# The end of a decoder layer on one core: read-back of routed rows ahead of the last pair's weights, its down weights by halves, three token tiles summed in PSUM, the last norm by halves on VectorE

## The chip, the cores and the metric

The kernel runs on one core of one Trainium2 chip. The metric is the time of one execution in device microseconds (us); the time of a kernel is the median of its runs.

## The reference

One decoder layer for 512 tokens of width 1024 in float32: a mixer (attention heads beside a short convolution), then a mixture of experts. The change touches only the end of the second part. Each token takes two of 32 experts (width 256), besides a shared expert that all tokens take; the sum is normed and added to the residual stream.

```python
a = jnp.einsum('nd,edf->nef', t, w_gate)
b = jnp.einsum('nd,edf->nef', t, w_up)
hid = jax.nn.silu(a) * b * combine[:, :, None]
routed = jnp.einsum('nef,efd->nd', hid, w_down)
shared = (jax.nn.silu(t @ w_sh_gate) * (t @ w_sh_up)) @ w_sh_down
ffn = routed + shared
h = h + rms_norm(ffn, post_ffn_norm)      # mean square over the 1024 columns, eps, gain
```

## The kernel before

The routed experts are worked off in 16 pairs (j, j+16), the loop of `pairs_gen` (L1445). A pair takes up to 64 tokens of each of its experts; the tokens' rows are gathered from HBM, transposed, and held as one 128-row tile. The weights of an expert are three loads of 1 MB: (e, 0) and (e, 1) hold the two halves of the depth of gate and up together, (e, 2) the down weights. `col2` (L1308) multiplies the two experts side by side, each in 64 of TensorE's columns. For one pair:

- gate and up: 16 float32 matmuls into the bank `pgu`, 8 for the loads (e, 0) and 8 for (e, 1);
- `hidden` (L1281): silu on ScalarE, then the product with the routing weight on VectorE; `hidden_t` (L1285): two transposes on TensorE (`pht`) and a copy on ScalarE; `xpose` (L1274): the next pair's rows transposed;
- `down` (L1515): 4 matmuls for each half of 512 columns, into `pdn`.

What follows differs. For the pairs ahead of `first = NP - PE_PAIRS` (L1444) the result is copied to `yb` and scattered by token to a DRAM buffer `y_d` (`send`, L1510, on POOL). `y_d` has two rows for each token and is read back at the end in four loads `kk0` to `kk3` of 1 MB, one for each tile c of 128 tokens. For the last `PE_PAIRS` pairs, 2 here, `y_out` (L1293) splits the result into a high and a low float32r part (`ys`: a copy on ScalarE, a subtraction on VectorE), and `combine` (L1297) multiplies both by a one-hot matrix `sel` into a bank `pcb`, which VectorE adds to the token's sum `acc(c)` (the tiles `sho`). So a pair's combination is 16 matmuls and 8 additions: 2 halves of the columns by 4 tiles.

`last_gen` (L1521) ends the kernel: it adds the read-back to `acc`, multiplies the last pair's down weights, and combines tile by tile. For the tiles in `INJ` (L47; only tile 3) the sum is not added by VectorE: `acc(c)` is put into a bank `pca` by a float32 matmul with the identity `ident`, and the two products with `sel` accumulate onto it. `post` (L1548) then takes, for each tile and half, the sum of squares on ScalarE and the product with the gain `gp` (into `tm`), which goes to VectorE or to GpSimd (G) by an estimate of the two engines' progress (`M_BIAS`, L1555). The power -0.5 runs on POOL, VectorE multiplies and adds the residual `hb`, and SP stores each half.

All weights pass through one ring of slots, and all their loads are issued by SP in the order of one list, written at L391 to L411:

```python
if j == NP - 1 and i == 2:
    queue_load("gp", g_post[None, :].to_broadcast([P, D]), D)
    for c in range(NT):
        queue_load(f"kk{c}", y_d[:, :].rearrange("(k c p) d -> c p k d", k=2, c=NT)[c],
                   ok=lambda: "sent" in cv)
for e in g:
    queue_load((e, i), we[e, i])
```

A load waits for the slot's last reader and for the landing of the load eight before it. On the other engines the order of the work is fixed when the program is built: generators yield until the builder's own clock (`Progress`) says that their inputs are there, and the one that can go on is taken, by priority. Each engine then runs its list in that order.

Of the kernel before, what the change touches and what calls it, by code (L numbers as in the profile page):

```python
# [46 lines left out]
INJ = (3,)  # L47
M_BIAS = 5.0
F_ALT = ()
# [9 lines left out]
PE_PAIRS = 2  # L59
# [109 lines left out]
def hymba_kernel(ctx: ExitStack, tc: tile.TileContext, xT, xmT, x, meta, cpk, pos, wqkv, wconv, wuq, wukv,  # L169
# [229 lines left out]
    for j, g in enumerate(pairs):  # L399
        for i in range(3):  # L400
            if j == NP - 1 and i == 2:
                queue_load("gp", g_post[None, :].to_broadcast([P, D]), D)
                for c in range(NT):
                    queue_load(f"kk{c}", y_d[:, :].rearrange("(k c p) d -> c p k d", k=2, c=NT)[c],
                               ok=lambda: "sent" in cv)
            for e in g:
                queue_load((e, i), we[e, i])
# [1025 lines left out]
    def pairs_gen():  # L1433
# [11 lines left out]
        for j, es in enumerate(pairs):  # L1445
            ps = None
            for i in range(2):
# [8 lines left out]
                rel(*w)  # L1456
            hidden(ps, wgt[:, j:j + 1], sg, hd)
# [11 lines left out]
            if j > first:  # L1469
                yield flag(sh, "done")  # L1470
                for c in range(NT):
                    yield every(at(ys), free_bank())
                    combine(ys, sel, HALF[0], c)
            yield every(at(hd), free_bank())
            hidden_t(hd, ht)
            if j > first:
                for c in range(NT):
                    yield free_bank()
                    combine(ys, sel, HALF[1], c)
# [8 lines left out]
            if j == NP - 1:  # L1488
                spawn(last_gen(es), 5)
                return  # L1490
# [16 lines left out]
            if j == first - 1:  # L1507
                cv["sent"] = True

# [11 lines left out]
    def last_gen(es):  # L1521
# [8 lines left out]
        for c in range(NT):  # L1530
            yield loaded(f"kk{c}")
            kk = got(f"kk{c}")
            for k in range(2):
                V.tensor_tensor(acc(c), acc(c), kk[:, k * D:(k + 1) * D], op=OP.add)
            rel(kk)
        yield every(loaded(*((e, 2) for e in es)), free_bank(2))
        w = [got((e, 2)) for e in es]
        yield at(*w, ht)
        for half in range(2):
            y_out(down(half, ht, [t[:, half * D:(half + 1) * D] for t in w]), ys, HALF[half])  # L1540
        rel(*w)
        yield loaded("hb0", "hb1")
        hb = [got("hb0"), got("hb1")]
# [4 lines left out]
        def post(c, pa):  # L1548
            a = [pa[q] if pa else acc(c)[:, HALF[q]] for q in range(2)]
            v, rc_ = var[:, 2 * c:2 * c + 2], rf[:, c:c + 1]  # L1550
            for q in range(2):
                yield at(a[q])
                k = 2 * c + q
                S.activation(rt["jk"], a[q], AF.Square, accum_out=ss[:, k:k + 1])
                t = max(PR.when(a[q], eng="DVE"), PR.t["DVE"]) + 0.6, max(PR.when(a[q], eng="POOL"), PR.t["POOL"]) + 1.3  # L1555
                (V if pa or t[0] + M_BIAS < t[1] else G).tensor_tensor(tmc(c, HALF[q]), a[q], gp[:, HALF[q]], op=OP.mult)
            yield at(ss[:, 2 * c:2 * c + 2])
# [3 lines left out]
            h = hb[c // 2][:, c % 2 * D:(c % 2 + 1) * D]  # L1561
            for q in HALF:
                yield at(rc_, tmc(c, q))
                if c in F_ALT:
                    S.activation(tmc(c, q), tmc(c, q), AF.Copy, scale=rc_)
                    G.tensor_tensor(h[:, q], tmc(c, q), h[:, q], op=OP.add)
                else:
                    V.scalar_tensor_tensor(h[:, q], tmc(c, q), rc_, h[:, q], op0=OP.mult, op1=OP.add)
                Y.dma_start(out[c * P:(c + 1) * P, q], h[:, q])
            if pa:  # L1570
                for q in range(2):
                    S.activation(acc(c)[:, HALF[q]], pa[q], AF.Copy)
                    held.remove(pa[q])

        for c in range(NT):
            pa = []
# [109 lines left out]
```

## Time and profile before

| | us |
|---|---|
| median of 3 runs (lowest to highest) | 526.93 (526.39 to 527.13) |
| the profiled execution | 526.53 |
| its span, first to last instruction | 524.7 |
| TensorE busy, share of the span | 476.8, 91% |
| VectorE | 230.9, 44% |
| ScalarE | 172.3, 33% |
| GpSimd (POOL) | 91.0, 17% |
| chain that ended last | TensorE 57%, DMA 30%, VectorE 9% |

The engines are PE (TensorE's matmuls), DVE (VectorE), ACT (ScalarE), POOL (GpSimd) and SP, which only issues DMAs. Every instruction of DVE, ACT, POOL and SP carries line L162, and every matmul L317, since helpers record them: the name of the tile tells what it is. Matmuls have two records for each float32 instruction. A row says who released an engine from idling in brackets, with the idle time.

### The profile page before, as it was taken

To read this page: it belongs to the slowest core of one execution; us is meant where nothing else is said; L and a number is where in the kernel's file an instruction comes from. 1 tells how busy PE (TensorE), PEld (TensorE's weight loads), DVE (VectorE), ACT (ScalarE), POOL (GpSimd) and SP (SyncE) were. 2 spreads that over 40 slices of the span, in tenths; PEclk is the share of its full clock that TensorE was granted. 3 is DMA by queue.
4 is the path that set the end of the run, shared out by engine and by line. 5 is a ranking of instruction groups with operands and counts; after the bars stand their busy time and mean duration, and the time that the engine had idled before them with its cause. 6 is when DMAs were issued, how large, how long until landed. Compare 5 with 4: busy or idle time off the path is not lost.

```text
span 524.7 us, 7250 instructions
## 1 busy us (share of the span) xinstructions
PE 476.8 (91%) x2754; PEld 302.9 (58%) x2754; DVE 230.9 (44%) x517; ACT 172.3 (33%) x351; POOL 91.0 (17%) x114
## 2 busy tenths in 40 slices
PE   7999999999999999889989999999999987787590
PEld 7998999788666888679933333343333332223230
DVE  6468789557778514778810000000000000001786
ACT  6754535444445633431041121221111111102041
POOL 1024333300001005420311110111111110000024
PEclk9999999999999999999999999999999999999886
DMA  8952240280127776399399999999999999999804
GB/s 291 400 214 80 81 161 0 106 298 30 52 81 253 297 277 276 152 402 362 133 403 417 420 422 420 421 419 422 418 419 419 416 412 408 417 392 397 342 24 162
DMA packets 30164, 151.06 MB, mean 288 GB/s; under 512 B 5392, under 2 KB 5776, under 8 KB 16048
## 3 DMA queue, kind: packets, MB, share of 16 engines
q1 hardware_dynamic: 25664, 142.63, 67.9%
q0 software_dynamic: 4320, 7.94, 4.1%
q8 instruction: 22, 0.36, 0.3%
q14 instruction: 14, 0.11, 0.1%
q10 hardware_dynamic: 144, 0.02, 0.0%
HBM read 140.54 MB, written 17.83 MB: 302 GB/s over the span
## 4 chain that ended last, share of the span: by engine, by line
PE 57%; DMA 30%; DVE 9%; issue 2%; ACT 1%; POOL 0%; DVEq 0%; SPq 0%; ACTq 0%
PE pc L317 13%; PE pgu L317 8%; DMA ld (11, 1)_3214<-in_we_dram 5%; DMA ld (12, 2)_3291<-in_we_dram 4%; PE pco L317 4%; DMA ld (8, 2)_3037<-in_we_dram 4%; PE pdn L317 4%; DMA ld (14, 0)_3393<-in_we_dram 4%; DMA ld (10, 0)_3133<-in_we_dram 4%; PE pq L317 4%; DMA ld (15, 1)_3474<-in_we_dram 4%; PE pS L317 4%; DMA ld (31, 2)_3584<-in_we_dram 4%; PE pO L317 3%; DVE rs L162 3%; PE psd L317 3%
## 5 line engine op out<-in xcount | busy, mean ns | idle before, releaser
L317 PE MATMUL pc<-xh,cw 128*128 128x256 f32 (+2 forms) x320 | 70.0, 309 | 0.0
L162 DVE SCALAR_TENSOR_TENSOR wk<-wk,wgt,pgu 128x256 f32<-128x256 f32 x16 | 7.7, 481 | 122.7 <-ACT wk L162 122.7
L317 PEld LDWEIGHTS pc<-xh,cw 128*128 128x128 f32 x320 | 52.3, 189 | 4.1 <-issue 1.3
L162 ACT ACTIVATE wk<-pgu 128x256 f32<-128x256 f32 x16 | 6.1, 383 | 139.0 <-PE pgu L317 139.0
L317 PE MATMUL pc<-xl,cw 128*128 128x256 f32 (+2 forms) x160 | 48.8, 305 | 0.0
L162 DVE COPY yb<-pdn 128x512 f32<-128x512 f32 x14 | 9.7, 692 | 79.6 <-PE pdn L317 79.6
L162 POOL DMA_INDIRECT xg<-t_d,idx x16 | 16.5, 1029 | 115.4 <-PE pxt L317 107.2
L317 PEld LDWEIGHTS pc<-xl,cw 128*128 128x128 f32 x160 | 30.3, 189 | 1.2
L162 ACT ACTIVATE att<-pS,nm 128x128 f32<-128x128 f32 (+3 forms) x32 | 16.9, 527 | 29.4 <-DVE nm L162 27.2
L162 POOL DMA_INDIRECT y_d<-yb,sidx x14 | 14.1, 1008 | 67.6 <-DVE yb L162 42.9
L317 PE MATMUL pS<-kT,qT 128*128 128x128 f32 (+3 forms) x64 | 22.7, 440 | 0.0
L162 POOL TENSOR_TENSOR sst<-rst,neghalf 128x1 f32<-128x1 f32 x12 | 6.5, 551 | 82.2 <-DVE rst L162 82.2
L317 PE MATMUL pco<-wo,cvh 128*128 128x512 f32 x64 | 20.6, 403 | 0.0
L317 PE MATMUL pao<-wo,mgh 128*128 128x512 f32 x64 | 20.2, 397 | 0.0
L162 POOL TENSOR_TENSOR cw<-ld conv,cw 128x1024 fp32r<-128x1024 f32 x6 | 15.7, 2624 | 18.4 <-ACT cw L162 18.4
L317 PE MATMUL psh<-tT,ld (32, 0)_1921 128*128 128x128 f32 x128 | 18.0, 279 | 0.0
L317 PE MATMUL pht<-ident,wk 128*128 128x128 f32 x32 | 6.8, 293 | 12.2 <-DVE wk L162 12.2
L317 PE MATMUL psh<-tT,ld (32, 1)_1923 128*128 128x128 f32 x128 | 17.8, 278 | 0.0
L317 PEld LDWEIGHTS pht<-ident,wk 128*128 128x128 f32 x32 | 3.5, 141 | 24.5 <-DVE wk L162 22.7
L162 ACT ACTIVATE wk<-pxt 128x512 f32<-128x512 f32 x32 | 17.4, 596 | 0.7
L162 ACT ACTIVATE m<-mix 128x512 bf16<-128x512 f32 (+1 forms) x12 | 9.3, 773 | 22.8 <-DVE mix L162 22.4
L317 PE MATMUL pxt<-ident,xg 128*128 128x128 f32 x128 | 16.6, 273 | 0.0
(487 smaller groups left out, 1221.9 us busy)
## 6 DMA issues: line engine op xcount, KB each, us to landing
ld conv<-in_wconv_dram SPq DMA_DIRECT2D x6, 1024.0 KB, 10.6
ld out<-in_wout_dram SPq DMA_DIRECT2D x4, 1024.0 KB, 5.7
y_d<-sel SPq DMA_DIRECT2D x4, 1024.0 KB, 8.1
ld kk<-y_d SPq DMA_DIRECT2D x4, 1024.0 KB, 18.8
xs<-in_x_dram SPq DMA_DIRECT2D x4, 512.0 KB, 9.5
x<-in_x_dram SPq DMA_DIRECT2D x4, 512.0 KB, 5.5
h_d<-mix SPq DMA_DIRECT2D x4, 512.0 KB, 2.8
t_d<-x SPq DMA_DIRECT2D x4, 512.0 KB, 2.6
```

What stands on the lines that cost most here:

```text
L162: r = f(*a, **k)
L317: f(o, *ins, **kw)
```

## The change

Five things are altered at the end of the kernel.

1. `PE_PAIRS` is 3: pair 13, too, is combined by matmuls, and is not scattered. The flag "sent" is set one pair earlier, and the read-back loads stand ahead of the four gate and up loads of pair 15. A new generator `back_gen` adds the read-back as it comes.
2. The combination of the pair before (16 matmuls) stands between the two halves of gate and up, no longer around the transposes.
3. The last pair's down weights come as two loads by halves of the columns, "dn" 0 and 1, both experts in each.
4. `INJ` is (1, 2, 3): three tiles are summed in PSUM, in six banks, with the six identity matmuls ahead of the down matmuls.
5. `last_gen` goes by halves: half 0 of all four tiles (combination, squares, product with the gain), then half 1, then norm and store. All eight products with the gain are on VectorE; POOL keeps the four powers.

```diff
-INJ = (3,)
-M_BIAS = 5.0
-F_ALT = ()
+INJ = (1, 2, 3)
...
-PE_PAIRS = 2
+PE_PAIRS = 3
...
-            if j == NP - 1 and i == 2:
-                queue_load("gp", g_post[None, :].to_broadcast([P, D]), D)
+            if j == NP - 1 and i == 0:
                 for c in range(NT):
                     queue_load(f"kk{c}", y_d[:, :].rearrange("(k c p) d -> c p k d", k=2, c=NT)[c],
                                ok=lambda: "sent" in cv)
+            if j == NP - 1 and i == 2:
+                queue_load("gp", g_post[None, :].to_broadcast([P, D]), D)
+
+                for half in range(2):
+                    queue_load(("dn", half), we[0:NE].rearrange("(a e) i p d -> e i p a d", a=2)[
+                        j, i, :, :, half * D:(half + 1) * D])
+                continue
...
                 rel(*w)
+                if j > first and i == 0:
+                    yield flag(sh, "done")
+                    for half in range(2):
+                        for c in range(NT):
+                            yield every(at(ys), free_bank())
+                            combine(ys, sel, HALF[half], c)
...
-            if j > first:
-                yield flag(sh, "done")
-                for c in range(NT):
-                    yield every(at(ys), free_bank())
-                    combine(ys, sel, HALF[0], c)
             yield every(at(hd), free_bank())
             hidden_t(hd, ht)
-            if j > first:
-                for c in range(NT):
-                    yield free_bank()
-                    combine(ys, sel, HALF[1], c)
...
             if j == first - 1:
                 cv["sent"] = True
+                spawn(back_gen(), 4)
...
+    def back_gen():
+
+        yield flag(sh, "done")
+        for c in range(NT):
+            yield loaded(f"kk{c}")
+            kk = got(f"kk{c}")
+            yield at(kk)
+            for k in range(2):
+                V.tensor_tensor(acc(c), acc(c), kk[:, k * D:(k + 1) * D], op=OP.add)
+            rel(kk)
+            cv["kk", c] = True
...
+        for c in range(NT):
+            yield flag(cv, ("kk", c))
+            if c in INJ:
+                for half in range(2):
+                    yield every(at(acc(c)[:, HALF[half]]), free_bank())
+                    pa[c, half] = bank("pca")
+                    held.append(pa[c, half])
+                    mm(pa[c, half], ident, acc(c)[:, HALF[half]], start=True, stop=False)
+
+        def part(c, q):
+            a = pa.get((c, q))
+            v = acc(c)[:, HALF[q]] if a is None else a
+            S.activation(rt["jk"], v, AF.Square, accum_out=ss[:, 2 * c + q:2 * c + q + 1])
+            V.tensor_tensor(tmc(c, HALF[q]), v, gp[:, HALF[q]], op=OP.mult)
+
+        def post(c):
...
+        for half in range(2):
+            o = HALF[half]
+            yield every(loaded(("dn", half)), free_bank())
+            w = got(("dn", half))
+            yield at(w, ht)
+            y_out(down(half, ht, [w[:, :D], w[:, D:2 * D]]), ys, o)
+            rel(w)
...
+            for c in range(NT):
                 yield every(at(ys[:, o], ys[:, D + o.start:D + o.stop]), free_bank())
                 if c in INJ:
                     for q in range(2):
+                        mm(pa[c, half], sel[:, c * P:(c + 1) * P], ys[:, q * D + o.start:q * D + o.stop], start=False,
                            stop=q == 1)
                 else:
                     combine(ys, sel, o, c)
+                part(c, half)
+                if half:
+                    post(c)
+                if half and c:
+                    store(c - 1)
+        store(NT - 1)
```

The list of SP's loads, from the first that differs, where (15, 0) is pair 15's first weights of expert 15 and `kk` the read-back. Before:

```order
L162 DMA ld (15, 0)_3458<-in_we_dram 128x2048
L162 DMA ld (31, 0)_3460<-in_we_dram 128x2048
L162 DMA ld (15, 1)_3474<-in_we_dram 128x2048
L162 DMA ld (31, 1)_3476<-in_we_dram 128x2048
L162 DMA ld gp<-in_g_post_dram 128x1024
L162 DMA ld kk_3574<-y_d 128x2x1024
L162 DMA ld kk_3576<-y_d 128x2x1024
L162 DMA ld kk_3578<-y_d 128x2x1024
L162 DMA ld kk_3580<-y_d 128x2x1024
L162 DMA ld (15, 2)_3582<-in_we_dram 128x2048
L162 DMA ld (31, 2)_3584<-in_we_dram 128x2048
```

And now:

```order
L160 DMA ld kk_3514<-y_d 128x2x1024
L160 DMA ld kk_3516<-y_d 128x2x1024
L160 DMA ld kk_3518<-y_d 128x2x1024
L160 DMA ld kk_3520<-y_d 128x2x1024
L160 DMA ld (15, 0)_3522<-in_we_dram 128x2048
L160 DMA ld (31, 0)_3524<-in_we_dram 128x2048
L160 DMA ld (15, 1)_3526<-in_we_dram 128x2048
L160 DMA ld (31, 1)_3528<-in_we_dram 128x2048
L160 DMA ld gp<-in_g_post_dram 128x1024
L160 DMA ld ('dn', 0)_3541<-in_we_dram 128x2x1024
L160 DMA ld ('dn', 1)_3551<-in_we_dram 128x2x1024
```

Four read-backs moved ahead of pair 15's gate and up loads, and the two down loads carry a half each.

TensorE's list at the last pair, where `pgu` is gate and up, `pcb` the combination, `pht` the transposes, `pdn` the down product. Before, from the last gate and up matmul:

```order
L317 MATMUL pgu<-ld (31, 1)_3476,wk 64x512
L317 MATMUL pcb<-ys,sel 128x512 x8
L317 MATMUL pht<-ident,wk 128x128 x2
L317 MATMUL pcb<-ys,sel 128x512 x8
L317 MATMUL pdn<-ld (15, 2)_3582,wk 64x512
L317 MATMUL pdn<-ld (31, 2)_3584,wk 64x512
```

Now, around the turn from the loads (15, 0) and (31, 0) to (15, 1) and (31, 1), where the two rows on either side alternate as often as before:

```order
L315 MATMUL pgu<-ld (15, 0)_3522,wk 64x512
L315 MATMUL pgu<-ld (31, 0)_3524,wk 64x512
L315 MATMUL pcb<-ys,sel 128x512 x16
L315 MATMUL pgu<-ld (15, 1)_3526,wk 64x512
L315 MATMUL pgu<-ld (31, 1)_3528,wk 64x512
```

And from the last gate and up matmul:

```order
L315 MATMUL pgu<-ld (31, 1)_3528,wk 64x512
L315 MATMUL pht<-ident,wk 128x128 x2
L315 MATMUL pca<-sho_2839,ident 128x512 x2
L315 MATMUL pca<-sho_2840,ident 128x512 x4
L315 MATMUL pdn<-ld ('dn', 0)_3541,wk 64x512 x4
L315 MATMUL pcb<-ys,sel 128x512 x2
L315 MATMUL pca<-ys,sel 128x512 x6
```

Sixteen `pcb` matmuls stand between the halves of gate and up, and six `pca` matmuls with `ident` between the transposes and the first down matmul.

VectorE's list from the last pair's split of its result (`ys`) on. Before:

```order
L162 TENSOR_TENSOR ys<-pdn,ys 128x512 x2
L162 TENSOR_TENSOR sho_2839<-pcb,sho_2839 128x512 x4
L162 TENSOR_TENSOR sho_2840<-pcb,sho_2840 128x512 x2
L162 TENSOR_SCALAR var<-ssf 128x1
L162 SCALAR_TENSOR_TENSOR var<-ssf,var 128x1
L162 TENSOR_SCALAR var<-ssf 128x1
L162 SCALAR_TENSOR_TENSOR var<-ssf,var 128x1
L162 TENSOR_TENSOR tm_3701<-sho_2840,ld gp 128x512
L162 SCALAR_TENSOR_TENSOR ld hb_3586<-tm_3700,rf,ld hb_3586 128x512 x2
L162 TENSOR_SCALAR var<-ssf 128x1
L162 SCALAR_TENSOR_TENSOR var<-ssf,var 128x1
L162 TENSOR_TENSOR tm_3701<-pca,ld gp 128x512 x2
```

Now:

```order
L160 TENSOR_TENSOR ys<-pdn,ys 128x512
L160 TENSOR_TENSOR sho_2839<-pcb,sho_2839 128x512
L160 TENSOR_TENSOR tm_3740<-sho_2839,ld gp 128x512
L160 TENSOR_TENSOR tm_3740<-pca,ld gp 128x512
L160 TENSOR_TENSOR tm_3741<-pca,ld gp 128x512 x2
L160 TENSOR_TENSOR ys<-pdn,ys 128x512
L160 TENSOR_TENSOR sho_2839<-pcb,sho_2839 128x512
L160 TENSOR_TENSOR tm_3740<-sho_2839,ld gp 128x512
L160 TENSOR_SCALAR var<-ssf 128x1
L160 SCALAR_TENSOR_TENSOR var<-ssf,var 128x1
L160 TENSOR_TENSOR tm_3740<-pca,ld gp 128x512
L160 TENSOR_SCALAR var<-ssf 128x1
```

Half 0 runs through all tiles' products (`tm`) ahead of the second split; what was six additions in a row is one in each half.

## Rows read from the trace of the kernel before

**Rows 1.** Page, part 2: GB/s in 40 slices of 13.1 us.

```profile
GB/s 291 400 214 80 81 161 0 106 298 30 52 81 253 297 277 276 152 402 362 133 403 417 420 422 420 421 419 422 418 419 419 416 412 408 417 392 397 342 24 162
```

**Rows 2.** Chain that ended last, from 440 us: start us, us, what.

```profile
482.13 18.66 DMA ld (31, 2)_3584<-in_we_dram
...
500.83 4.30 PE pdn L317 x14
```

**Rows 3.** Timeline of SP, from 400 us: start us, us, queue, line, tiles.

```profile
456.04 0.33 SPq L162 DMA_DIRECT2D ld (15, 0)_3458<-in_we_dram  x1
...
472.37 5.92 SPq L162 DMA_DIRECT2D ld kk<-y_d  x4
```

**Rows 4.** Timeline of POOL, same stretch: the last two scatters.

```profile
446.88 1.01 POOL L162 DMA_INDIRECT y_d<-yb,sidx  x1 [3.84 <-issue]
463.90 0.99 POOL L162 DMA_INDIRECT y_d<-yb,sidx  x1 [16.01 <-DVE yb L162]
```

**Rows 5.** Windows: PE, PEld, DVE, ACT, POOL busy; clock, DMA share, GB/s.

```profile
472.00:474.00 2.00, 1.01 (x9) 0.92 (x9) 1.08 (x2) 0.76 (x2) 0.00 (x0) 1.00 0.80 291
...
496.00:500.00 4.00, 1.53 (x2) 0.29 (x2) 3.97 (x4) 0.00 (x0) 0.00 (x0) 0.50 0.31 128
```

**Rows 6.** Timeline of TensorE, 479 to 512 us: start, us, instruction.

```profile
479.61 0.64 PE L317 MATMUL pgu<-ld (31, 0)_3460,wk 128*64 128x512 f32 x1 [0.78 <-DMA ld (31, 0)_3460<-in_we_dram]
...
482.67 0.59 PE L317 MATMUL pgu<-ld (31, 0)_3460,wk 128*64 128x512 f32 x1
...
484.61 0.64 PE L317 MATMUL pgu<-ld (31, 1)_3476,wk 128*64 128x512 f32 x1 [1.34 <-DMA ld (31, 1)_3476<-in_we_dram]
...
487.23 1.02 PE L317 MATMUL pgu<-ld (31, 1)_3476,wk 128*64 128x512 f32 x2
488.18 2.13 PE L317 MATMUL pcb<-ys,sel 128*128 128x512 f32 x8
...
490.29 2.11 PE L317 MATMUL pcb<-ys,sel 128*128 128x512 f32 x8
498.47 1.94 PE L317 MATMUL pdn<-ld (15, 2)_3582,wk 128*64 128x512 f32 x2 [6.07 <-DMA ld (15, 2)_3582<-in_we_dram]
500.83 1.12 PE L317 MATMUL pdn<-ld (31, 2)_3584,wk 128*64 128x512 f32 x1 [0.42 <-DMA ld (31, 2)_3584<-in_we_dram]
...
501.74 0.80 PE L317 MATMUL pdn<-ld (31, 2)_3584,wk 128*64 128x512 f32 x1
...
508.73 1.02 PE L317 MATMUL pca<-sho,ident 128*128 128x512 f32 x2
...
510.05 1.02 PE L317 MATMUL pca<-sho,ident 128*128 128x512 f32 x2
```

**Rows 7.** Timeline of VectorE, 488 us to the end.

```profile
488.71 0.48 DVE L162 SCALAR_TENSOR_TENSOR wk<-wk,wgt,pgu 128x256 f32<-128x256 f32 x1 [9.10 <-ACT wk L162]
...
494.49 9.66 DVE L162 TENSOR_TENSOR sho<-sho,ld kk 128x1024 f32<-128x1024 f32 x8
504.07 0.69 DVE L162 TENSOR_TENSOR ys<-pdn,ys 128x512 fp32r<-128x512 f32 x1
...
506.39 3.75 DVE L162 TENSOR_TENSOR sho<-pcb,sho 128x512 f32<-128x512 f32 x6
...
511.37 3.42 DVE L162 SCALAR_TENSOR_TENSOR ld hb<-tm,rf,ld hb 128x512 f32<-128x512 f32 x2
...
515.04 1.28 DVE L162 TENSOR_TENSOR tm<-pca,ld gp 128x512 f32<-128x512 f32 x2
...
516.52 4.05 DVE L162 SCALAR_TENSOR_TENSOR ld hb<-tm,rf,ld hb 128x512 f32<-128x512 f32 x6
```

**Rows 8.** Timeline of ScalarE, the same stretch.

```profile
511.63 0.60 ACT L162 ACTIVATE wk<-pca 128x512 bf16<-128x512 f32 x1
...
512.36 0.60 ACT L162 ACTIVATE wk<-pca 128x512 bf16<-128x512 f32 x1
...
515.76 1.20 ACT L162 ACTIVATE sho<-pca 128x512 f32<-128x512 f32 x2 [2.72 <-DVE tm L162]
```

More of the change, by code (lines that the diff above doesn't have):

```diff
@@ L1488, in pairs_gen @@
             if j == NP - 1:
-                spawn(last_gen(es), 5)
+                spawn(last_gen(), 5)
                 return
@@ L1519, in down, with last_gen @@
         return ps
-    def last_gen(es):
+    def back_gen():
[8 more added lines that the diff above has]
+            cv["kk", c] = True
+    def last_gen():
         ys, ht = rt["ys"], rt["wk"][:, D + 512:D + 768]
@@ L1529, in last_gen @@
         fin.update(gp=gp, tm=tm)
[L1530 to L1543, printed above, removed]
+        pa = {}
         def tmc(c, o=slice(0, D)):
             return tm[c // 2][:, c % 2 * D:(c % 2 + 1) * D][:, o]
-        def post(c, pa):
-            a = [pa[q] if pa else acc(c)[:, HALF[q]] for q in range(2)]
-            v, rc_ = var[:, 2 * c:2 * c + 2], rf[:, c:c + 1]
[L1551 to L1557, printed above, removed]
+        for c in range(NT):
[12 more added lines that the diff above has]
+        def post(c):
+            v, rc_ = var[:, 2 * c:2 * c + 2], rf[:, c:c + 1]
             V.tensor_scalar(v[:, 0:1], ss[:, 2 * c:2 * c + 1], 1.0 / D, EPS, op0=OP.mult, op1=OP.add)
@@ L1560, in post, with store @@
             G.tensor_tensor(rc_, v[:, 1:2], neghalf[:, 0:1], op=OP.pow)
-            h = hb[c // 2][:, c % 2 * D:(c % 2 + 1) * D]
+        def store(c):
+            rc_, h = rf[:, c:c + 1], hb[c // 2][:, c % 2 * D:(c % 2 + 1) * D]
             for q in HALF:
[L1563 to L1568, printed above, removed]
-                Y.dma_start(out[c * P:(c + 1) * P, q], h[:, q])
[L1570 to L1576, printed above, removed]
-            for half in range(2):
-                o = HALF[half]
-                if c in INJ:
-                    yield every(at(acc(c)[:, o]), free_bank(2))
-                    pa.append(bank("pca"))
-                    held.append(pa[half])
-                    mm(pa[half], ident, acc(c)[:, o], start=True, stop=False)
+                V.scalar_tensor_tensor(h[:, q], tmc(c, q), rc_, h[:, q], op0=OP.mult, op1=OP.add)
+                Y.dma_start(out[c * P:(c + 1) * P, q], h[:, q])
+        for half in range(2):
[6 more added lines that the diff above has]
+            if half:
+                yield loaded("hb0", "hb1")
+                hb = [got("hb0"), got("hb1")]
+            for c in range(NT):
                 yield every(at(ys[:, o], ys[:, D + o.start:D + o.stop]), free_bank())
@@ L1586, in last_gen @@
                     for q in range(2):
-                        mm(pa[half], sel[:, c * P:(c + 1) * P], ys[:, q * D + o.start:q * D + o.stop], start=False,
+                        mm(pa[c, half], sel[:, c * P:(c + 1) * P], ys[:, q * D + o.start:q * D + o.stop], start=False,
                            stop=q == 1)
@@ L1590, in last_gen @@
                     combine(ys, sel, o, c)
-            spawn(post(c, pa), 4)
+                part(c, half)
+                if half:
+                    post(c)
+                if half and c:
+                    store(c - 1)
+        store(NT - 1)
+        for (c, q), a in pa.items():
+            S.activation(acc(c)[:, HALF[q]], a, AF.Copy)
+            held.remove(a)
     spawn(r_gen(), 0)
```

## The prediction

> **What bounds the kernel now.** The page's bandwidth line comes first. From slice 21 (262 us) to slice 37 (485 us) the transfers run at 392 to 422 GB/s, and two slices later they have nearly stopped [rows 1]: for 220 us the loads of weights are the bound, and what they leave is a short tail. The chain of waits says the same: a load that was issued when the eighth before it had landed, then the down matmuls of the last pair [rows 2]. So the end of the kernel has two parts: when the last weights are there, and what is left to do behind them. Of the first, the timeline of TensorE shows how far it keeps up: it starts on (31, 0) at 479.61, as that lands, on (31, 1) at 484.61, idles 6.07 us ahead of (15, 2) at 498.47, and starts on (31, 2) at 500.83 [rows 6]. Behind them lie 23.9 us to the end of the span at 524.7; VectorE works through most of them [rows 7]. The question for the change is whether TensorE still waits for the down weights, or they for it.
>
> **Loads.** Two loads take 484.61 - 479.61 = 5.0 us, 2.5 each; the five and a half from (31, 1) to (15, 2) (gp is half a load, the read-backs are four) take 13.86, or 2.52 each [rows 6]. A read-back thus costs as much as weights. Pair 13's scatter goes; it moved as many bytes as half a load, so some 1.25 us of the same bandwidth (an estimate; the bounds are nothing, if it fitted into gaps, and 2.5). Its own place in POOL's list frees nothing, since POOL idles around it. Pair 15's gate and up loads now stand behind four read-backs: (31, 0) lands at 479.61 + 4 x 2.5 - 1.25 = 488.4, (31, 1) at 493.4. The down halves come behind gp: before, (31, 2) was there at 500.83, so now dn 0 at 497.1 and dn 1 at 499.6.
>
> Does the read-back wait at the head of SP's list for its scatter? Before, pair 13's scatter was issued at 463.90 and the first read-back went out 8.5 us later [rows 3, 4]. Now it follows pair 12's, issued at 446.88; plus 8.5 that is 455.4, and its turn comes where (15, 0) went out, at 456.04 [rows 3]. No wait, with 0.6 us to spare.
>
> **Work ahead of the last pair.** VectorE's list has the first read-back (landing where (15, 0) did less 1.25, near 476) ahead of pair 14's hidden product, which so comes near 478.8, some 6 us later than without. I cost it at nothing: pair 14's transposes and eight down steps, some 5 us, then run until about 484, and (31, 0) is only there at 488.4. The eight read-back additions took 9.66 us on VectorE, ending at 504.15, when the first split could begin [rows 7]; now they end by about 488. That removal frees little: from 500.83 the half's four steps, the first of 0.91, and ScalarE's copy of 0.60 would not have let the split begin before 504 [rows 6, 8].
>
> **The last pair on TensorE.** From (31, 0)'s landing everything is in one list:
> - rest of the first half of gate and up: from 479.61 to the step after the one at 482.67, each step 0.43, 3.5 us [rows 6]: 491.9;
> - 16 combination matmuls: from 488.18 to 490.29 lie eight of them and two transposes of 0.07, so 0.245 each [rows 6], 3.9 us: 495.8. VectorE's eight additions (3.75 for six [rows 7]) end some 1 us later, and TensorE's next work does not wait for them;
> - second half of gate and up: all its loads are there, eight steps, as from 484.61 to the end at 488.25, 3.6 us [rows 6]: 499.4;
> - silu and product, from 488.25 to 489.19, 0.95 us [rows 6, 7], and the transposes, 0.3: 500.65;
> - six identity matmuls, float32, two records each that start 0.43 apart: 510.05 - 508.73 = 1.32 us is one of them with two products (0.46), so 0.86 each [rows 6], 5.1 us: 505.75;
> - the down matmuls of half 0: four steps to the end, 1.9 us: 507.65.
>
> The whole takes 19.3 us and begins with a landing, so the down weights lie ready 8.7 us before they are used. Before, the same combination and transposes had been done in the wait for the down weights, and the identity matmuls came behind them for one tile only. Copy and split of half 0 (0.60 and 0.69 with 0.07 of hand-over) end at 509.0; before, that was 504.07 + 0.69 = 504.76 [rows 7]. **4.2 us late.**
>
> **The tail.** From the split of half 0, at A = 509.0. Combination and addition need 0.55 and 0.6. Then ScalarE has four squares, starting 0.73 apart [rows 8], 3.0 us with the last one's accumulator read, and behind them the copy of half 1, 0.6; VectorE's four products with the gain (0.64 each [rows 7]) fit beside that. The second split ends at A + 5.5. Half 1 runs tile by tile: addition and first product to 1.85, the first square done at 2.0, tile 1's product to 3.35 and its norm to 3.65; tile 0's two final products at 0.675 (six in 4.05 [rows 7]) to 5.0; tile 2's product, norm, and tile 1's final products to 7.25; tile 3's to 8.15; the last four final products to 10.9. So VectorE ends at A + 16.4 = 525.4, against 520.57 before, 15.8 behind the first split [rows 7]. What leaves it: four additions, 2.4 us, and the two final products that took 3.42 together instead of 1.35 while POOL had its products; what comes: five products, 3.2 us, and the waits by halves. Behind the last product 524.7 - 520.57 = 4.1 us for the store and the end, as before. End: 529.5, or **4.8 us late**.
>
> In this tail the six products from PSUM wait for ScalarE's square of the same bank. A row shows that readers of a bank follow one another: the copies out of `pca` start at 515.76, as VectorE's first product out of it ends (515.04, 0.68 long), after 2.72 us of idling [rows 7, 8]. The Trainium skill, PSUM — Partial Sum Buffer, section "PSUM bank collisions raise a hardware error", has the rule that two engines must not access one bank at once, two readers included, so that such pairs are ordered; the trace agrees, and by that rule squares and products of the three PSUM tiles can't overlap, which speaks against summing there. If they could, tile 1's product would come 0.55 us sooner and the sum would be 4.2 instead of 4.8.
>
> **The sum.** Against the profiled execution: 526.53 + 4.8 = 531.3. It lies 0.4 below the median of the runs shown, so between 531.3 and 531.7: I say 531.4. Bounds of this case: the scatter from 0 to 2.5 us (+1.25, -1.25), the combination from 0.235 to 0.27 a matmul (0.6), the tail from the 15.8 of before to 17.5 (-0.6, +1.1); from about 529 to 533.5.
>
> **Rivals.**
> 1. *TensorE keeps up, and the landing of the down weights still decides* (the other side: faster). The place is the first down matmul; it decides if TensorE needs less than 8.7 us from (31, 0) to there instead of 17.3. Then half 0 starts at 497.1, is split at 500.4, and the end is at 500.4 + 16.4 + 4.1 = 520.9: 522.7 us. For it: until the last pair, TensorE waits for nearly every load [rows 6]. Against it: each term above is a row of the same instructions, and they are in one list. A part of it (read-backs that land faster than weights, the six identity matmuls in a gap) gives something between.
> 2. *The clock falls as well.* From 496 to 500, after TensorE's 6 us of idling, the granted clock was 0.50, the level of 1.2 GHz instead of 2.4 [rows 5], and a step took 0.91 (500.83 to 501.74) instead of 0.43 [rows 6]. Now TensorE idles some 4 us ahead of pair 14's transposes and again, with a few steps between, from 484 to 488.4. If the first eight steps of the last pair run at the low level, that is 7 x 0.47 = 3.3 us more on the same list: 534.7. For it: the idle time; against it: it is in pieces.
> 3. *The move of the read-back fails at SP*: pair 12's scatter lands late, and the list behind it stands. Before, SP so waited 4 us, and bandwidth fell to 291 GB/s from 420 for 2 us [rows 5] and less beside it, about 1 us lost: 532.4.
> 4. *Nothing comes of it*: gains and losses within a microsecond of each other, 527.
>
> **Chances.** 0.65 for the forecast, 0.11 for the first rival and what lies between it and no change, 0.12 for the second, 0.07 for the third, 0.05 for none. A change of less than 0.2% (1.05 us) can't be told from none. The forecast and rivals two and three lie above 528: slower 0.84; the first is faster, 0.11; the fourth the same, 0.05. The range leaves out the first rival and reaches to the second: 527.5 to 535.0; the forecast's own is 529 to 533.5.
>
> **What would show it.** In the profile after: (31, 0) is first multiplied near 488.4 and (31, 1) has no wait for its load; six `pca` matmuls with `ident` stand between the transposes and the first down matmul, and that starts near 505.8 with no DMA as its releaser; the chain goes through TensorE from (31, 0) on; the first split ends near 509.0, and VectorE near 525.4. If instead the first down matmul waits for dn 0 or dn 1, the forecast is wrong and the first rival right; if it starts above 508 with a clock of 0.5 near 490, the second; if SP's read-back waits for the scatter, the third.

## The result, and the profile after

The changed kernel takes 532.14 us (median of 5, 531.58 to 534.13), the kernel before 526.93 in the same comparison: a ratio of 1.0098, with a 95% interval of 1.0078 to 1.0117. It is slower, by about 5.2 us, and 0.7 us above the 531.4 forecast.

The profiled execution of the changed kernel took 534.13 us, 2 us more than its median. From 232 to 237 us its granted clock was 0.66 on average, where the profile of before has 1.00. Until 248 us SP's loads go out within 0.1 us of those before; at 263 us they are 1.4 us late, and the load of (30, 0), issued at 441.51 before, goes out at 443.13, 1.62 us late. To compare a time of after with one of before or with the prediction, take 1.62 us off.

The page of after, the bandwidth line of part 2 and the engine line of part 4 (the chain that ended last):

```profile
GB/s 289 400 203 79 80 159 1 147 250 80 1 100 309 292 280 225 191 420 337 104 418 417 422 420 426 418 418 421 421 418 417 411 411 409 410 385 414 174 1 160
PE 74%; DMA 12%; DVE 9%; ACT 2%; issue 2%; POOL 0%; DVEq 0%; SPq 0%; ACTq 0%
```

From slice 21 to slice 37 the transfers run at 385 to 426 GB/s, much as in [rows 1]; but slices 38 and 39 have 174 and 1 where before there were 342 and 24. The slices are not equally wide (13.3 us here, 13.1 before), so the size is better taken from the issue of (30, 0): dn 1, the last weights, lands 58.2 us behind it (482.73 + 18.6 - 443.13, rows below), where (31, 2) landed 59.3 behind it before (482.13 + 18.66 in [rows 2], less 441.51). The loads are through 1.1 us earlier, and the kernel ends later. The chain from 472 us (start us, us, what) shows what lies between:

```profile
472.02 18.14 DMA ld (31, 0)_3524<-in_we_dram
490.20 3.65 PE pgu L315 x14
493.85 3.95 PE pcb L315 x16
497.79 3.61 PE pgu L315 x16
...
502.38 0.44 PE pht L315 x2
502.82 5.15 PE pca L315 x12
507.97 1.89 PE pdn L315 x8
509.88 0.60 ACT ys L160
510.51 0.70 DVE ys L160
```

In [rows 2] the chain's last load was (31, 2), and only the down matmuls stood between it and the tail. Now the last load in the chain is (31, 0), and 19.6 us of TensorE's list follow it. The timeline of TensorE has no DMA as releaser of the first down matmul, and the DMA view of the same stretch (KB each, us from issue to landing) says why:

```profile
502.65 5.32 PE L315 MATMUL pca<-sho,ident 128*128 128x512 f32 x12
507.90 1.51 PE L315 MATMUL pdn<-ld ('dn', 0)_3541,wk 128*64 128x512 f32 x6
```

```profile
ld ('dn', 0)_3541<-in_we_dram SPq DMA_DIRECT2D x1, 1024.0 KB, 18.6
ld ('dn', 1)_3551<-in_we_dram SPq DMA_DIRECT2D x1, 1024.0 KB, 18.6
```

SP's timeline (start us, us) gives the issue to which this is added:

```profile
457.70 9.87 SPq L160 DMA_DIRECT2D ld kk<-y_d  x4
467.66 4.26 SPq L160 DMA_DIRECT2D ld (15, 0)_3522<-in_we_dram  x1
...
480.19 0.38 SPq L160 DMA_DIRECT2D ld ('dn', 0)_3541<-in_we_dram  x1
482.73 0.38 SPq L160 DMA_DIRECT2D ld ('dn', 1)_3551<-in_we_dram  x1
```

dn 0 was issued at 480.19 and landed 18.6 us later, at 498.8; it lay ready for 9.1 us. VectorE's timeline has the tail, which in [rows 7] began with a split at 504.07:

```profile
510.51 0.69 DVE L160 TENSOR_TENSOR ys<-pdn,ys 128x512 fp32r<-128x512 f32 x1 [7.59 <-ACT ys L160]
...
512.52 0.69 DVE L160 TENSOR_TENSOR tm<-sho,ld gp 128x512 f32<-128x512 f32 x1
514.00 2.13 DVE L160 TENSOR_TENSOR tm<-pca,ld gp 128x512 f32<-128x512 f32 x3 [0.78 <-ACT wk L160]
516.04 0.68 DVE L160 TENSOR_TENSOR ys<-pdn,ys 128x512 fp32r<-128x512 f32 x1
...
524.85 2.74 DVE L160 SCALAR_TENSOR_TENSOR ld hb<-tm,rf,ld hb 128x512 f32<-128x512 f32 x4
```

VectorE waits 7.59 us for the first split, and its last product ends at 524.85 + 2.74 = 527.59.

### The profile page after: what moved, and what is told of

The parts are those of the page before. It is cut to its first block, busy times and chain, and to the rows that moved or that the text cites. A ratio compares the mean times of both kernels' runs of the same rounds, so it can differ in the third digit from the quotient of the medians.

```text
span 532.2 us, 7305 instructions
## 1 busy us (share of the span) xinstructions
PE 486.4 (91%) x2778; PEld 308.3 (58%) x2778; DVE 236.2 (44%) x528; ACT 174.9 (33%) x356; POOL 83.8 (16%) x108
## 4 chain that ended last, share of the span: by engine, by line
PE 74%; DMA 12%; DVE 9%; ACT 2%; issue 2%; POOL 0%; DVEq 0%; SPq 0%; ACTq 0%
PE pgu L315 17%; PE pc L315 13%; PE pdn L315 7%; DMA ld (28, 1)_3281<-in_we_dram 4%; PE pco L315 4%; DMA ld (30, 0)_3395<-in_we_dram 4%; PE pq L315 4%; PE pS L315 4%; DMA ld (31, 0)_3524<-in_we_dram 3%; PE pO L315 3%; DVE rs L160 3%; PE psd L315 3%; PE pqh L315 2%; PE pao L315 2%; PE psh L315 2%; PE pT L315 2%
## 5 line engine op out<-in xcount | busy, mean ns | idle before, releaser
L160 POOL DMA_INDIRECT xg<-t_d,idx x16 | 16.4, 1025 | 117.1 <-PE pxt L315 102.0
L160 POOL DMA_INDIRECT y_d<-yb,sidx x13 | 13.1, 1009 | 51.7 <-issue 28.6
```

Source lines behind the costliest of these rows:

```text
L160: r = f(*a, **k)
```

## The experiments

Every run stands beside runs of the kernel before on its own chip (medians of before 526.93 to 527.37), so ratios are compared. The three columns on the right take one profiled execution apart: from the issue of (30, 0) to the end of the first split (the landing of the weights and the work behind it), from there to the end of VectorE's last product (the tail), and from there to the end of the span (the last store). The first of them is free of what the clock did earlier in that execution.

| kernel | median us | ratio to before [95%] | (30, 0) to first split | to last product | to the end |
|---|---|---|---|---|---|
| before | 526.93 | 1 | 63.25 | 15.81 | 4.1 |
| after | 532.14 | 1.0098 [1.0078, 1.0117] | 68.07 | 16.39 | 4.6 |
| e11: tail of before | 527.59 | 1.0009 [0.9996, 1.0022] | 63.45 | 16.06 | 4.2 |
| e2: no identity matmuls | 527.46 | 1.0007 [0.9989, 1.0025] | 63.53 | 16.38 | 4.6 |
| e5: identity behind down | 529.30 | 1.0034 [1.0018, 1.0049] | 63.50 | 17.84 | 4.7 |
| e4: one tile in PSUM | 532.46 | 1.0077 [1.0052, 1.0103] | 66.32 | 18.69 | 4.6 |
| e3: combination late | 532.55 | 1.0088 [1.0065, 1.0111] | 68.25 | 16.39 | 4.6 |
| e1: read-back behind | 527.63 | 1.0003 [0.9988, 1.0019] | 63.72 | 16.36 | 4.6 |
| e6: e1 and e5 | 524.85 | 0.9946 [0.9925, 0.9966] | 60.03 | 16.88 | 4.6 |
| e7: e6, two pairs | 525.17 | 0.9960 [0.9942, 0.9978] | 60.37 | 16.89 | 4.7 |
| e8: before, three pairs | 525.71 | 0.9961 [0.9947, 0.9975] | 62.58 | 15.74 | 4.2 |
| e10: two read-backs ahead, halves | 525.11 | 0.9959 [0.9946, 0.9973] | 60.36 | 16.88 | 4.7 |
| e9: the same, tail of before | 524.38 | 0.9958 [0.9943, 0.9974] | 60.75 | 16.38 | 4.1 |
| e12: e9 with filled waits | 523.04 | 0.9925 [0.9906, 0.9943] | 59.35 | 16.23 | 4.2 |

### What in TensorE's list costs the time: e2, e3, e4, e11, e5

**e2** leaves the six identity matmuls out; the sums of tiles 1 to 3 so lack what `acc` held before the last pair.

```diff
-                    mm(pa[c, half], ident, acc(c)[:, HALF[half]], start=True, stop=False)
...
-                        mm(pa[c, half], sel[:, c * P:(c + 1) * P], ys[:, q * D + o.start:q * D + o.stop], start=False,
+                        mm(pa[c, half], sel[:, c * P:(c + 1) * P], ys[:, q * D + o.start:q * D + o.stop], start=q == 0,
```

> The six identity matmuls are left out of the change, so the sums of tiles 1 to 3 lack all but the last pair's part. Theory: they lie on the list between (31, 0) and the first down matmul, 12 records of 0.43 = 5.15 us, and the down weights of half 0 lie ready 9.1 us before they are used, so all of it comes off: 527.0 us (526.5 to 527.5). Rival, the down weights' landing sets the start: no change, 532. Rival, VectorE's list in the tail sets the end whatever TensorE does: under 2 us less, 530 to 532.

Measured: 1.0007, so 0.0091 x 527 = 4.8 us less than after. Of the 5.15 us the list is 4.5 shorter, since TensorE now waits some 0.5 us for ScalarE's copy of the transposes (`wk` in its chain). The loss is gone, and the tail is what it was: beyond that half microsecond no other wait took its place.

```profile
500.03 0.45 PE pht L315 x2
...
500.57 0.39 ACT wk L160
...
501.00 1.96 PE pdn L315 x8
```

**e3** puts the combination of pair 14 back around pair 15's transposes.

```diff
-                if j > first and i == 0:
-                    yield flag(sh, "done")
-                    for half in range(2):
-                        for c in range(NT):
-                            yield every(at(ys), free_bank())
-                            combine(ys, sel, HALF[half], c)
```

> One part undone: the combination of the pair before stands around the transposes again, 8 matmuls on either side, instead of 16 between the halves of gate and up. Theory: between (31, 0) and the identity matmuls TensorE does the same work, 1.5 us of waiting for (31, 1) comes in and 0.95 us of silu and product is covered: no difference, 531.5 to 533. Rival, a combination in the middle of gate and up delays them by its 3.9 us and that is the cost: 528.5.

Measured: 1.0088; the intervals lie over each other. Where the 16 matmuls stand makes no difference that shows. The 1.5 us of waiting for (31, 1) isn't in the profile, but a low clock is in its place: 0.50 from 486 to 490 us, and the two halves of gate and up take 8.67 us without a wait between them, 1.4 more than the 3.65 + 3.61 of after.

**e4** sums tile 3 alone in PSUM.

```diff
-INJ = (1, 2, 3)
+INJ = (3,)
```

> One part undone: only tile 3 is summed in PSUM, tiles 1 and 2 are added by VectorE. Theory: four identity matmuls less on the list, 3.4 us, against four more additions of 0.6 on VectorE in the tail (2.4), less some 0.2 of waits for squares of the same bank: about 1 us less, 531 (530.3 to 531.8). Rival, sums in PSUM cost nothing since they stand in a wait: 2.2 us more, 534.3. Rival, the order of squares and products of one bank is the cost: 3 us less or more, 529 or below.

Measured: 1.0077 against 1.0098, so 1.1 us less than after, the size expected; but the intervals overlap and the median, 532.46, lies above the 530.3 to 531.8 given, so the gain can't be told from none. The first half of the trade is there: four identity matmuls fewer, and in the profile the first split comes 1.75 us sooner. It would have been 3.4, but in that execution the clock was low at the last pair's first half, which took 5.34 us in place of 3.65. The second half is there too: VectorE has the additions of tiles 1 and 2 back, and its tail is 18.69 long instead of 16.39. Summing a tile in PSUM takes 1.15 us from VectorE and gives 1.7 to TensorE. That is a gain only where TensorE waits anyway.

**e11** undoes the tail alone: from the transposes on the kernel is as before, except that the down weights come by halves.

```diff
-INJ = (1, 2, 3)
+INJ = (3,)
+M_BIAS = 5.0
+F_ALT = ()
...
+        for c in range(NT):
+            yield flag(cv, ("kk", c))
+        for half in range(2):
+            yield every(loaded(("dn", half)), free_bank())
+            w = got(("dn", half))
+            yield at(w, ht)
+            y_out(down(half, ht, [w[:, :D], w[:, D:2 * D]]), ys, HALF[half])
+            rel(w)
...
```

> The changed kernel with its tail alone undone: behind the transposes come the down matmuls of both halves at once, one tile summed in PSUM, and the norm of whole rows with VectorE and GpSimd, as before; loads, read-back, combination and the down weights by halves stay as changed. Theory (the identity matmuls ahead of the first down matmul are the loss, and the tail by halves gains nothing behind it): the first down matmul starts 5.1 us sooner and the end lies 15.8 + 4.1 us behind the first split, as in the kernel before: time near 526.5 (525.5 to 527.8), as before the change. Rival (the loads put in front of pair 15's weights are the loss): 530 or more.

Measured: 1.0009, as the theory had it. Its chain has the steps of after's, without the one of 5.15 us between the transposes and the down matmuls:

```profile
497.73 3.61 PE pgu L317 x16
...
502.32 0.45 PE pht L317 x2
...
503.29 3.68 PE pdn L317 x16
```

So the changed loads with the old tail are no worse than the kernel before, and no better: TensorE, not the landing, now sets the start of the down matmuls, at nearly the same time.

**e5** keeps the six identity matmuls and moves them behind the down matmuls of their half.

```diff
-                    mm(pa[c, half], ident, acc(c)[:, HALF[half]], start=True, stop=False)
...
+            for c in (1, 2):
+                if (c, half) not in pa:
+                    yield from identity(c, half)
             for c in range(NT):
+                if c == 2 and (3, half) not in pa:
+                    yield from identity(3, half)
                 yield every(at(ys[:, o], ys[:, D + o.start:D + o.stop]), free_bank())
```

> The changed kernel with one thing moved: the six identity matmuls stand behind the down matmuls of their half (tiles 1 and 2 straight behind them, tile 3 behind tile 1's combination) instead of between the transposes and the first down matmul. Theory (TensorE's one list from (31, 0) on is the bound, and the down weights lie ready): the first down matmul starts 5.1 us sooner, as the transposes end, and what comes back is 0.3 us in which two identity matmuls outlast copy and split. Time near 527.4 (526.5 to 528.3). Rival (the down weights or the tail set the end, TensorE's list is only the chain that ended last): the down matmuls wait for dn 0, the time stays above 530.

Measured: 529.3, 1.9 above the expected 527.4; of 4.8 us 0.0064 x 527 = 3.4 are gained. The first split does come sooner by the predicted amount (63.50 against 68.07), but the tail grows by 1.45 us. I had taken the identity matmuls for hidden behind ScalarE, all but 0.3 us. The chain shows them in the way:

```profile
503.35 1.91 PE pca L316 x4
505.26 0.47 PE pcb L316 x2
505.73 2.26 PE pca L316 x8
507.98 1.87 PE pdn L316 x8
509.85 1.92 PE pca L316 x4
511.76 0.48 PE pcb L316 x2
```

The half-1 down matmuls end at 509.85, since three identity matmuls of half 0 stand ahead of them in the list, and the second split ends 6.5 us behind the first instead of 5.5 in after. The first combination of half 1 comes at 511.76, since two more outlast copy and split: the other 0.5.

### The loads: e1, e6, e7, e8

**e1** queues the read-backs behind pair 15's gate and up weights; the first is added inside pair 15, the others behind its hidden product.

```diff
-            if j == NP - 1 and i == 0:
+            if j == NP - 1 and i == 2:
                 for c in range(NT):
...
+                    if j == NP - 1:
+                        spawn(back_gen(), 4)
+                        yield flag(cv, ("kk", 0))
```

> One part undone: the four read-back loads stand behind pair 15's gate and up loads again; the rest of the change stays. (The additions of the read-back stand later on VectorE too, tile 0's behind pair 14's combination, the others behind pair 15's hidden product, so that no product waits for a read-back.) Theory, TensorE's list behind the landing of (31, 0) sets the end: (31, 0) lands 10 us sooner, the list is through its combination and transposes before the down weights are there, and the last read-back addition, near 498, and tile 3's two identity matmuls set the first down matmul at about 499.5, A at 502.7: about 525 us, 7 less than the change. Rival, the tail by halves costs it (all products on VectorE, squares and products of one bank in turn): the tail is the same, so within 1 us of the change, 531 to 533. Rival, the identity matmuls alone cost it: they still stand ahead of the down matmuls, so 530 or more.

Measured: 527.63, a gain of 0.0095 x 527 = 5.0 us over after, where 7 were expected. The chain and VectorE's timeline show where the rest went:

```profile
480.54 3.43 PE pgu L315 x16
...
494.88 7.08 PE pca L315 x12
501.95 1.89 PE pdn L315 x8
```

```profile
489.46 2.47 DVE L160 TENSOR_TENSOR sho<-sho,ld kk 128x1024 f32<-128x1024 f32 x2
...
492.35 7.26 DVE L160 TENSOR_TENSOR sho<-sho,ld kk 128x1024 f32<-128x1024 f32 x6
```

The identity matmuls, which need the read-backs added, start at 494.88 when the second one is, and take 7.08 us instead of 5.15: VectorE's additions run until 499.61, and the clock was low from 494.8 to 498.3. Besides, TensorE came to pair 15 at 480.54 and found its first weights there, because it had pair 13 to combine inside pair 14 as well. A part of the wait had moved from the loads to VectorE and TensorE.

**e6** is e1 with the identity matmuls of tiles 2 and 3 behind the down matmuls, those of tile 1 ahead (the list of what stands ahead is `((1, 0), (1, 1))`).

> Read-back loads behind pair 15's gate and up, and the identity matmuls of tiles 2 and 3 behind the down matmuls of their half (those of tile 1 fill the wait for dn 0). Theory: with both causes gone the first down matmul waits for dn 0 (landing near 497), the split of half 0 ends near 500.5, the tail by halves takes 16.4 to 16.7 from there and 4.6 to the end: span 521.5, time 523.3 (522.3 to 525): faster than both kernels. Rival (VectorE, which adds the read-backs until 499.6 and then builds the last selection, holds the split): time 525 or more.

Measured: 524.85, inside the range given, and below both kernels. The way there was not the expected one: its first down matmul doesn't wait for dn 0 but for tile 1's identity matmuls, and these for VectorE, which adds the read-backs (rows under e7); so far the rival was right. The two losses add up within their intervals: 3.4 us for the place of the identity matmuls (e5) and 5.0 for the place of the read-backs (e1) make 8.4, and e6 gains 0.0152 x 527 = 8.0.

**e7** is e6 with `PE_PAIRS = 2`.

> The same with two pairs combined on TensorE instead of three, so that pair 13 goes through the scatter and the read-back again. Theory: the scatter's half load comes back in the stream and dn 0 lands 1.25 us later, while TensorE, without the combination inside pair 14, no longer falls behind the loads; since dn 0 is waited for, the time is 1.25 us above the kernel with three pairs: 524.5. Rival (TensorE's lag counts for more than the scatter): the same time or below.

Measured: 525.17; the intervals of e6 and e7 overlap, and the 1.25 us expected between them didn't show. dn 0 does land later: its first down matmul waits for it until 497.74, 57.1 us behind the issue of (30, 0), against 55.7 in e9. But in e6 the matmul isn't waiting for dn 0; it starts at 499.77 in the chain, 56.8 behind that issue, because two identity matmuls wait 1.95 us for VectorE and then run at the low clock. The timeline of e6:

```profile
493.99 0.44 PE L316 MATMUL pht<-ident,wk 128*128 128x128 f32 x2 [1.00 <-DVE wk L161]
496.38 3.38 PE L316 MATMUL pca<-sho,ident 128*128 128x512 f32 x4 [1.95 <-DVE sho L161]
499.70 1.94 PE L316 MATMUL pdn<-ld ('dn', 0)_3541,wk 128*64 128x512 f32 x8
```

**e8** changes one number in the kernel before.

```diff
-PE_PAIRS = 2
+PE_PAIRS = 3
```

> The kernel before with the one number changed that combines three pairs on TensorE instead of two. Theory: the scatter of pair 13 costs the stream 1.25 us, which is gained, and the combination inside pair 14 lies in TensorE's waits: 525.7 (525 to 526.5). If the scatter fitted into gaps, or the combination makes TensorE late for pair 15, no change: 526.9 or more.

Measured: 0.9961, a gain of 1.3 to 2.8 us by the interval. Its chain has the term itself:

```profile
480.88 18.61 DMA ld (31, 2)_3551<-in_we_dram
...
499.54 4.82 PE pdn L317 x14
```

(30, 0) was issued at 441.49, as before, and (31, 2) is multiplied at 499.54 instead of 500.83 [rows 2]: 1.29 us for the scatter of pair 13. In this profile 0.67 of them reach the first split (62.58 against 63.25), because these down matmuls, which start sooner, run longer at the low clock (0.51 from 498 to 502 us) and take 4.82 us instead of 4.30. This one number pays without the rest of the change. It isn't the only part that pays: e7 does without it and is at 0.9960 too. There half 0's down matmuls start 57.1 us behind the issue of (30, 0), as dn 0 lands, while before they needed (31, 2), multiplied 59.3 behind it. That points to the down weights by halves, which no run here changes alone.

### The tail and the clock: e9, e10, e12

**e9** and **e10** load two read-backs ahead of pair 15's second half of gate and up and two behind it, combine three pairs and take the down weights by halves; e9 has the tail of before, as in e11, e10 that by halves, as in e6. The lines against e6:

```diff
-            if j == NP - 1 and i == 2:
-                for c in range(NT):
+            if j == NP - 1 and i:
+                for c in range(2 * i - 2, 2 * i):
```

> Two read-backs ahead of pair 15's second half of gate and up and two behind it, three pairs combined on TensorE, down weights by halves, and the tail of the kernel before. Theory: (31, 1) lands near 488.4, TensorE is through with the transposes near 496, VectorE with the read-back additions near 500.4, dn 0 lands near 497; the first split ends near 501, the tail takes 15.8 and 4.1 from there: span 520.9, time 522.7 (521.7 to 524.2), the best of all kernels here. Rival (VectorE's list, with the first two read-backs ahead of pair 15's hidden product, holds the transposes and so the down matmuls): first split after 503, time 525 or more.

> The same loads with the tail by halves (three tiles summed in PSUM, the identity matmuls of tile 1 in the wait for dn 0, the others behind the down matmuls of their half). Theory: the first split ends near 501 too, and from there the tail takes 16.9 and 4.6 us, as read from the run with both causes gone: span 522.5, time 524.3, so 1.6 above its twin with the tail of before. Rival (the tail by halves is worth what it was made for once nothing holds the first split): time below its twin.

Measured: 0.9958 and 0.9959 (medians 0.7 us apart), no difference that can be told from none, where 1.6 us was expected between them, and e9 1.7 above its 522.7. In the profiles the tail by halves is the longer one, by 0.5 us to the last product and 0.5 behind it. What e9 loses ahead of that is the clock: TensorE idles from 491.9 to 494.6, runs two transposes, and idles again to 497.04; e9's window from 496 to 500 us (PE, PEld, DVE, ACT, POOL busy; clock, DMA share, GB/s) and its timeline say the rest.

```profile
496.00:500.00 4.00, 2.96 (x8) 1.13 (x10) 3.91 (x4) 0.00 (x0) 0.00 (x0) 0.50 0.24 96
```

```profile
497.04 3.68 PE L317 MATMUL pdn<-ld ('dn', 0)_3541,wk 128*64 128x512 f32 x8 [1.92 <-DMA ld ('dn', 0)_3541<-in_we_dram]
500.48 2.49 PE L317 MATMUL pdn<-ld ('dn', 1)_3551,wk 128*64 128x512 f32 x8
```

At 1.2 GHz the first half takes 3.68 us; at 2.4 it took 1.94 in e6. In e10 tile 1's identity matmuls stand in that wait. They take the low clock (0.57 from 496.0 to 499.2 us), and the down matmuls behind them run at 2.4 GHz (1.00 from there to 501.1):

```profile
496.09 3.12 PE pca L316 x4
499.21 1.89 PE pdn L316 x8
```

**e12** fills these two waits in e9 with work whose product nothing uses.

```diff
+    def fill(n):
+        ps = bank("pfl")
+        for _ in range(n):
+            mm(ps, ident, rt["wk"][:, :512], start=True, stop=True)
+        S.activation(rt["jk"][:, :1], ps[:, :1], AF.Copy)
...
+            if j == NP - 1:
+                fill(4)
             yield every(at(hd), free_bank())
             hidden_t(hd, ht)
+            if j == NP - 1:
+                fill(2)
```

> The kernel with two read-backs ahead of pair 15's second half and the tail of before (its profile: TensorE idles from 491.9 to 494.6 and from 495.1 to 497.0, the granted clock is 0.50 from 496 to 500, and the four steps of half 0 take 3.68 us instead of 1.89), with six float32 matmuls of 0.86 us put into these two waits, four and two, into a bank that nothing uses: work added, nothing else changed. Theory (the low clock costs what its rows show): at the full clock half 0 is multiplied in 1.9 us, the first split ends near 500.7 instead of 502.1, the second near 502.7 instead of 504.3; the time falls by 1.6, to 522.8 (522 to 523.8). Rival (the clock falls for another reason, or the added work delays the transposes and the down matmuls by as much): no change or up to 1 us slower, 524.4 to 525.4.

Measured: 523.04, ratio 0.9925: the expected gain, and the fastest kernel of this study, 4.0 us (0.0075 x 527) below the kernel before. Its window and timeline at the same place:

```profile
496.00:500.00 4.00, 3.80 (x15) 1.02 (x15) 3.94 (x5) 0.77 (x2) 0.00 (x0) 1.00 0.21 85
```

```profile
491.49 3.70 PE L317 MATMUL pfl<-wk,ident 128*128 128x512 f32 x8
495.03 0.38 PE L317 MATMUL pht<-ident,wk 128*128 128x128 f32 x2
495.25 1.88 PE L317 MATMUL pfl<-wk,ident 128*128 128x512 f32 x4
497.06 1.94 PE L317 MATMUL pdn<-ld ('dn', 0)_3541,wk 128*64 128x512 f32 x8
```

The first down matmul starts when it did; it runs at 2.4 GHz. The intervals of e9 and e12 meet at 0.9943, so the size of the gain is known to about a microsecond, and its cause by the rows. The granted clock of the whole execution bears it out beyond the two profiles: 0.987 to 0.991 in e12's six, 0.980 to 0.983 in six of e9's seven and 0.989 in the other.

## Why the prediction was right

**The mechanism.** The prediction was that TensorE's one list from (31, 0) takes the place of the down weights as the bound. The chain of after shows it, e2 and e11 take the identity matmuls out of the list and the loss goes, and in e1, which starts the list sooner, it goes too.

**The landings.** With 1.62 us off, (31, 0) is multiplied at 488.6 (forecast 488.4), and dn 0 lands at 497.2 (497.1). The read-backs cost as much as weights, and the scatter of pair 13 cost 1.29 us in e8 (estimate 1.25, bounds 0 and 2.5). Pair 14's transposes and down steps, costed at nothing, were done at 486.1 (487.72 less 1.62) where 484 was said; of the 4.4 us of slack 2.5 were left, so the term held.

**SP and the scatter.** The first read-back was issued 3.2 us behind (30, 2), the spacing that (15, 0) had there before. Rival 3 did not come about.

**TensorE's list.** 19.3 us were forecast from (31, 0) to the end of the half's down matmuls, and 19.66 are in the chain: first half 3.65 (3.5), combination 3.95 (3.9), second half 3.61 (3.6), silu, product and transposes 1.42 (1.25), identity 5.15 (5.1), down 1.89 (1.9). The first split stands 4.82 us later than before, where 4.2 was said: 0.4 of the difference are steps taken too short, mostly the first half and the stretch of silu and transposes, and 0.2 the landing of (31, 0).

**The tail.** A + 16.4 was forecast, 16.39 measured, and the second split ends at A + 5.5 in both. In it the products of PSUM tiles wait for the squares of the same bank: the product of tile 0, which lies in SBUF, starts with its square at 512.52, the first one out of `pca` at 514.00, when the square's accumulator has been read. This is the order that the Trainium skill, PSUM — Partial Sum Buffer, section "PSUM bank collisions raise a hardware error", asks for; the trace agrees, and the program's semaphores are what keeps it.

**The mis-sized term** is the end: 4.1 us behind the last product were taken over from before, and 4.6 are there, in all runs with the tail by halves (4.6 to 4.7) and in none with the old one (4.1 to 4.2). The last store is issued as the last product ends in both, and the difference is its landing: 2.6 us after the issue in after, while no store of before took over 2.1. From 529.34 to 529.84, 1.75 to 2.25 us behind the last product, the transfers of after still have a share of 0.06 at 25 GB/s, as much as one engine of 16 is; in the same stretch before, 522.32 to 522.82, there are none. Why it is late stays open. With the 0.6 of the first split this makes a trace 5.9 us longer instead of 4.8. The medians lie 5.2 apart, since the profiled execution of before is 0.4 below its median and that of after, with 1.62 off, 0.4 above; that the forecast of 531.4 missed the median by only 0.7 is in part luck.

**The other rivals.** The clock (rival 2) fell in after too, but from 478.5 to 485.3, on pair 14's transposes and down steps, which were done at 487.7, with (31, 0) still to come at 490.2. In e4's profile it fell on the last pair's first half and cost 1.7 us, about half of the 3.3 in the rival. Rival 1 needed TensorE to reach the down matmuls before dn 0 landed, and rival 4 needed gains and losses to cancel; dn 0 lay ready for 9.1 us, since the steps of TensorE's list add up as they were read from before.

## What to carry to other kernels

When loads are reordered, count what TensorE still has to do behind each landing: a load that is moved ahead makes the weights behind it late, all the work on them then stands in one list, and work that was free in the wait for the last load is free no longer. Sums moved from VectorE to TensorE with an identity matmul cost 1.7 us a tile here for 1.15 saved, so they can pay only where TensorE waits anyway; behind the last weights' matmuls (e5) they still made the tail 1.45 us longer. And a change of several edits is worth taking apart: here a single number was worth some 2 us alone, while the change as a whole lost 5.

## What the hardware showed unexpectedly

- **The place of a clock drop moves between executions and builds.** Before, it lay at 495 to 502 us; in after at 478.5 to 485.3 and, in this execution, once more near 233 (its mean granted clock is 0.982, that of after's four other executions 0.985 to 0.988). From 232 to 237 us TensorE was 94% busy (4.70 of 5 us) in both kernels, and from 229 to 231, just ahead, for 0.64 of 2 us in both; the clock fell in one and not in the other. Profiles of e6 and e11 have the same 0.66 from 232 to 237 us, the others have 1.00. In the three with it (30, 0) goes out at 442.97 to 443.14, in the others at 440.66 to 442.08. So single profiled executions are compared from a common event near the end.
- **Work that nothing uses paid.** Six matmuls of 0.86 us in idle stretches kept the granted clock at 1.00 (e12) and shortened the down matmuls behind them from 3.68 to 1.94 us. Of the 14 profiles only e12's has a granted clock of 1.00 all the way from 440 to 500 us.
- **Loads issued behind the read-backs hold SP.** Issues of the weight loads ahead of them take 0.33 us each in after; the one of (15, 0) behind four read-backs took 4.26, and the next two 1.14 and 1.15. (Before, (15, 2) went out 1.3 us behind the fourth read-back's issue and took 0.34.) From 470 to 474 us the transfers ran at 334 GB/s, beside 416 and more in the next 8 us. It cost nothing that shows: (31, 0) was there within 0.2 us of the forecast.
